# Keeping the second parts of the input projection's weights in DRAM between the two halves of a decoder stack

## The chip, the core and the metric

The kernel runs on one core of one Trainium2 chip. What counts is the device time of one execution in microseconds. Of the kernel before there are three timed runs, 1667.75, 1672.88 and 1679.4 us, with the median 1672.88 us, and one profiled execution of 1675.07 us, whose span in the trace is 1673.3 us.

## What is computed

Two decoder layers run over a prompt of 512 tokens and, beside it, 8 sequences of 4 new tokens each (32 columns more). Per layer the reference does this:

```
h = rms_norm(x, g_mix_pre)
p_rw, p_s5, p_gdn, p_swa = split(h @ w_in)        # the input projection, 1024 -> 2824
o = [rwkv7(p_rw), s5(p_s5), gated_delta(p_gdn), window_attention(p_swa)]
x = x + rms_norm(concat(o) @ w_out, g_mix_post)
h = rms_norm(x, g_mlp_pre)
x = x + rms_norm(square(relu(h @ w_up)) @ w_down, g_mlp_post)
```

All is float32. The four mixers carry state from token to token; the states are outputs too.

## The kernel before, in words

The 544 columns are worked in two halves: half 0 has 256 prompt columns, half 1 the other 256 and the 32 new ones (288 columns). Features lie on the 128 partitions. Half 1 of a layer needs the mixers' states that half 0 left, so the order of the program is: input projection of half 0, mixers of half 0, input projection of half 1, output projection of half 0, mixers of half 1, MLP of half 0, and so on through both layers (`body`, L1787 on). Work of different stages is interleaved.

Every dense product is made exact enough by splitting both operands into a first part `hi` (the value rounded to the type that TensorE takes, float32r) and a second part `lo` (what is left). Three products are summed: hi by hi, hi by lo, lo by hi. For the weights the split is done on the way in, by `load_part` (L1652): a piece of 128 rows by 4 by 128 weights (256 KB) is loaded into a `wraw` buffer by SP's DMA queue (L1658), ScalarE (ACT) casts it into `whi` (through L231), and VectorE (DVE) subtracts `whi` from `wraw` into `wlo` (through L235). There are 5 buffers for `wraw`, and 3 each for `whi` and `wlo`. A unit of 128 output features takes two such pieces and 24 matmuls: for each piece 4 with `whi` by the activations' first part, 4 with `whi` by their second part, and 4 with `wlo` by their first part (`dense`, L1699; matmuls are L219).

The input projection (`project`, L1852) has 22 such units and one narrow one per layer and half, so its 44 pieces are loaded and split four times in the program: layers 0 and 1, halves 0 and 1. Each half loads and splits the same weights anew.

Each unit's result is taken out of PSUM by code of its own mixer. For the first 8 units (`rw_evac`, L367 on) GpSimd (POOL) copies a column into the buffer (L381, L382), ACT copies the result out of PSUM, and POOL keeps the last column in `rwlast` (L398) and another piece in `rwshs` (L386). POOL also adds up squares for the norms (`sums`, L235), and issues some output DMAs from its own queue.

No order is written by hand. The program is recorded in the order of the code, and a scheduler in the build, which times the program by a simulation of its own and takes the priorities in `PRIO` into account, decides in which order the instructions stand on each engine. On the chip each engine, and SP's and POOL's DMA issues among them, goes through its own list in order.

Of the kernel before, what the change touches and what calls it, by code (L numbers as in the profile page):

```python
# [9 lines left out]
F32 = mybir.dt.float32  # L10
F32R = mybir.dt.float32r
# [5 lines left out]
DEPTH, D, SEQ, DB, DS = 2, 1024, 512, 8, 4  # L17
# [121 lines left out]
class K:  # L139
# [1509 lines left out]
        self.nc.sync.dma_start(out=self.x[half], in_=src)  # L1649
        return new  # L1650

    def load_part(self, src):  # L1652

        m = src.shape[-1]
        raw = self.t([128, 4, 128], "wraw", bufs=5)[:, :, :m]
        hi = self.t([128, 4, 128], "whi", bufs=3, dt=F32R)[:, :, :m]
        lo = self.t([128, 4, 128], "wlo", bufs=3, dt=F32R)[:, :, :m]
        d = self.nc.sync.dma_start(out=raw, in_=src)  # L1658
        self.after(d, self.last_load)
        self.last_load = d.ins  # L1660
        self.loads += 1
        if self.loads == FIRST_LOADS:
            for w in self.waiting:
                self.after(w, d.ins)
        self.acopy(hi, raw)
        self.tt(lo, raw, hi.bitcast(F32), ALU.subtract)
        return hi, lo

    def later(self, f):
# [26 lines left out]
        while self.pending:  # L1696
            self.pending.pop(0)()

    def dense(self, units, half, rhs, evac):  # L1699

        n = HALVES[half][1]
        rh, rl = rhs
        for j, (key, src) in enumerate(units):
            if j in (1, 2) and self.pending:
                self.pending.pop(0)()
            ps = self.ps([128, n], "mm")[:src.shape[-1]]
            i = 0
            for k0 in (0, 4):
                with self.ahead("load"):
                    hi, lo = self.load_part(src[:, k0:k0 + 4])  # L1710
                for a, b in ((hi, rh), (hi, rl), (lo, rh)):
                    for k in range(4):
                        self.mm(ps, a[:, k], b[:, k0 + k], i == 0, i == 23)
                        i += 1
            with self.ahead("evac"):
                evac(key, ps)
# [70 lines left out]
    def body(self):  # L1787
        self.pool("sb")
        self.pool("psum", space=PSUM)
        self.pool("dram", space=DRAM)  # L1790
        self.x = [self.i["xT"][:, :, c0:c0 + n] for c0, n in HALVES]
        self.last_layer = False
        self.carry = [{} for _ in range(DEPTH)]
        self.mix = {}
        self.last_gd = None
        self.mean = self.t([128, 1], "mean")
        self.nc.gpsimd.memset(self.mean, 1.0 / D)
        self.eps = self.t([128, 1], "eps")
        self.nc.gpsimd.memset(self.eps, NORM_EPS)
        self.nc.scalar.preload_act_table_set("natural_log_exp_and_others")  # L1800
        h = self.first(0)
        self.tables(0)

        a, b = (self.w([128, 2304], "f9") for _ in range(2))
        xs = self.w([128, 2048], "acc")
        self.alt = dict(xs=xs, cv=a[:, 0:1536], sv=a[:, 1536:1792], gz=b[:, 0:512], us=b[:, 512:1024], sx=b[:, 1024:1792],
                        ba=b[:, 1792:2048])
        r = self.project(0, 0, h)
        zero = self.w([128, 520], "r4")
        self.nc.gpsimd.memset(zero, 0.0)  # L1810
        self.diag = []
        for w in range(2):
            self.diag.append([self.t([64 * 1040], f"diag{w}{x}", pool="dram") for x in range(2)])
            for d in self.diag[w]:
                self.nc.gpsimd.dma_start(out=d.rearrange("(p f) -> p f", p=128), in_=zero)
        self.alt = None
        h = self.first(1)
        self.mixers(r)
        for l in range(DEPTH):
            self.pf = self.pfs[l]  # L1820
            self.last_layer = l == DEPTH - 1
            if not l:
                r = self.project(l, 1, h)
                x = self.out_proj(l, 0)
            else:
                x = self.out_proj(l, 0)
                self.flush()
                r = self.project(l, 1, h["h"])
            self.mixers(r)
            xb = []  # L1830
            other = lambda: xb.append(self.out_proj(l, 1))
            h = self.mlp(l, 0, x, other if l == DEPTH - 1 else None)
            if not xb:
                other()
                self.flush()
            x = xb[0]
            if l + 1 < DEPTH:
                self.tables(l + 1)
                self.pf = self.pfs[l + 1]
                r = self.project(l + 1, 0, h["h"])  # L1840
                self.mixers(r)
                self.pf = self.pfs[l]
            h = self.mlp(l, 1, x)
        self.flush()
# [6 lines left out]

    def project(self, l, half, h):  # L1852
        def proj(us, evac):
            self.dense([(u, self.unit("w_in", l, u)) for u in us], half, h, evac)

        with self.section("rwin"):
            rw = self.rw_begin(l, half)
            proj(range(0, 8), lambda u, ps: self.rw_evac(rw, u, ps))
        with self.section("gdin"):
            gd = self.gd_begin(l, half)  # L1860
            proj((10, 11, 12, 13, 14, 15), lambda u, ps: self.gd_evac(gd, u - 10, ps))
            self.narrow(self.i["w_ba"][l].rearrange("p (k m) -> p k m", k=8), half, h, lambda ps: self.gd_evac_ba(gd, ps))
            proj((16, 17), lambda u, ps: self.gd_evac_z(gd, u - 16, ps))
        with self.section("swin", bank="mm"):
            sw = self.sw_begin(l, half)
            proj((18, 19, 20, 21), lambda u, ps: self.sw_evac(sw, u - 18, ps))
        with self.section("s5in"):
            s5 = self.s5_begin(l, half)
            proj((8, 9), lambda u, ps: self.s5_evac(s5, u - 8, ps))
            us = s5["us"]  # L1870
            s5["sc"] = self.t([256, 4, s5["N"]], f"s5su{half}", pool="dram", bufs=2)
            self.nc.sync.dma_start(out=s5["sc"].rearrange("(u p) j c -> p u (j c)", u=2), in_=us.rearrange("p u j c -> p u (j c)"))
        return dict(l=l, half=half, rw=rw, gd=gd, sw=sw, s5=s5)
# [160 lines left out]
```

## Time and the profile before

| | |
|---|---|
| median of three runs | 1672.88 us |
| profiled execution | 1675.07 us, span 1673.3 us |
| TensorE busy in matmuls (PE) | 1576.6 us, 94% of the span |
| weight loads of TensorE (PEld) | 1472.2 us, 88% |
| VectorE (DVE) | 1245.0 us, 74% |
| ScalarE (ACT) | 952.2 us, 57% |
| GpSimd (POOL) | 373.9 us, 22% |
| DMA | 275.21 MB, 164 GB/s on the mean |

Busy times are those of instructions; a matmul's end is modelled, since matmuls are pipelined. The four input projections lie at about 2 to 112 us (layer 0, half 0), 112 to 250 us (layer 0, half 1), 640 to 725 us (layer 1, half 0) and 1033 to 1119 us (layer 1, half 1), by the starts of the loads `wraw<-in_w_in` in SP's queue.

### The profile page before, as it was taken

What the parts mean: (1) busy time and instruction counts of PE and PEld (TensorE: products, weight loads), DVE (VectorE), ACT (ScalarE), POOL (GpSimd) and SP (SyncE); (2) the same over time, 40 slices, a digit from 0 to 9 for tenths busy, and PEclk for the clock granted to TensorE, in tenths of its full rate; (3) what the DMA queues carried; (4) which work ended last, traced back from release to release, by engine and by line L of the source; (5) the groups of instructions that cost most, each with busy time, mean ns of one, the idle gap of its engine ahead of it and who ended that gap; (6) DMA issues with size and microseconds to landing.
All of it is one profiled execution on the core that took longest, in us unless ns stands there. A gap on an engine that the chain in (4) does not pass through costs nothing. (4 is left out here: it accounts for less than half of the span.)

```text
span 1673.3 us, 38301 instructions
## 1 busy us (share of the span) xinstructions
PE 1576.6 (94%) x14098; PEld 1472.2 (88%) x14098; DVE 1245.0 (74%) x3067; ACT 952.2 (57%) x2096; POOL 373.9 (22%) x689
## 2 busy tenths in 40 slices
PE   6988998789999999989999998999999999899996
PEld 6877987679898999879989998989899899899996
DVE  7888675876696868898576667989778865966665
ACT  5676556744346467765453556886444456655543
POOL 6561142200122614530001004530002101400002
PEclk9998998879999999999999999999999899999998
DMA  6634453343467557736346455535544765555452
GB/s 219 221 120 118 140 165 123 108 119 117 135 189 252 179 170 231 234 105 167 106 152 196 165 179 191 172 126 144 145 140 146 234 209 187 194 189 166 160 169 98
DMA packets 210184, 275.21 MB, mean 164 GB/s; under 512 B 78266, under 2 KB 101116, under 8 KB 209580
## 3 DMA queue, kind: packets, MB, share of 16 engines
q1 hardware_dynamic: 208076, 266.59, 50.8%
q0 software_dynamic: 1920, 6.17, 1.0%
q8 instruction: 110, 1.80, 0.4%
q14 instruction: 78, 0.64, 0.1%
HBM read 243.20 MB, written 31.21 MB: 164 GB/s over the span
## 5 line engine op out<-in xcount | busy, mean ns | idle before, releaser
L231 ACT CAST whi<-wraw 128x512 fp32r<-128x512 f32 x752 | 463.5, 619 | 439.3 <-PE ps L219 268.4
L235 DVE TENSOR_TENSOR wlo<-wraw,whi 128x512 fp32r<-128x512 f32 x752 | 545.7, 730 | 198.5 <-ACT whi L231 171.3
L219 PE MATMUL ps<-h,whi 128*128 128x288 f32 (+1 forms) x3264 | 518.6, 299 | 20.1 <-ACT h L231 17.8
L219 PEld LDWEIGHTS ps<-h,whi 128*128 128x128 f32 x3264 | 455.4, 194 | 35.2 <-ACT h L231 22.1
L219 PE MATMUL ps<-f,whi 128*128 128x288 f32 (+1 forms) x2752 | 425.6, 294 | 9.6 <-ACT whi L231 4.7
L219 PEld LDWEIGHTS ps<-f,whi 128*128 128x128 f32 x2752 | 374.4, 190 | 22.4 <-ACT whi L231 6.8
L219 PE MATMUL ps<-h,wlo 128*128 128x288 f32 (+1 forms) x1632 | 291.0, 298 | 7.4 <-DVE wlo L235 6.8
L219 PEld LDWEIGHTS ps<-h,wlo 128*128 128x128 f32 x1632 | 238.7, 193 | 16.1 <-DVE wlo L235 11.2
L219 PE MATMUL ps<-f,wlo 128*128 128x288 f32 (+1 forms) x1376 | 238.7, 293 | 3.3 <-DVE wlo L235 3.1
L235 POOL TENSOR_TENSOR sums<-sums,d 128x288 f32<-128x288 f32 (+1 forms) x105 | 101.8, 970 | 548.9 <-ACT d L227 541.0
L219 PEld LDWEIGHTS ps<-f,wlo 128*128 128x128 f32 x1376 | 197.4, 190 | 8.5 <-DVE wlo L235 4.6
L219 PE MATMUL ps<-r,r 128*128 128x72 f32 (+7 forms) x800 | 90.0, 281 | 4.5 <-DVE r L235 2.6
L219 PEld LDWEIGHTS ps<-r,r 128*128 128x128 f32 (+4 forms) x800 | 72.3, 175 | 11.0 <-DVE r L235 3.3
L235 DVE TENSOR_TENSOR acc<-acc,ps 128x256 f32<-128x256 f32 (+1 forms) x96 | 41.7, 434 | 49.5 <-PE ps L219 49.1
L231 ACT CAST f<-d 128x256 fp32r<-128x256 f32 (+1 forms) x136 | 56.6, 416 | 29.1 <-DVE d L235 28.5
L227 ACT ACTIVATE d<-acc 128x288 f32<-128x288 f32 (+1 forms) x109 | 46.2, 431 | 34.5 <-DVE acc L235 20.9
L235 DVE TENSOR_TENSOR f<-d,f 128x256 fp32r<-128x256 f32 (+1 forms) x136 | 59.1, 436 | 6.8 <-ACT f L231 6.7
L235 DVE TENSOR_TENSOR d<-d 128x288 f32<-128x288 f32 (+1 forms) x128 | 58.1, 454 | 0.7 <-ACT d L227 0.7
L227 ACT ACT_TABLE_LOAD x43 | 55.2, 1283 | 0.8
L227 ACT ACTIVATE d<-ps 128x288 f32<-128x288 f32 (+1 forms) x128 | 50.4, 394 | 8.8 <-PE ps L219 8.0
L244 DVE SCALAR_TENSOR_TENSOR d<-acc,pf,sums 128x256 f32<-128x256 f32 (+1 forms) x80 | 39.7, 507 | 6.2 <-ACT sums L227 4.9
L231 ACT COPY r<-ps 64x128 f32<-64x128 f32 (+2 forms) x60 | 22.7, 383 | 27.3 <-PE ps L624 11.4
(381 smaller groups left out, 1861.9 us busy)
## 6 DMA issues: line engine op xcount, KB each, us to landing
wraw<-in_w_up SPq DMA_DIRECT2D x256, 256.0 KB, 2.8
wraw<-in_w_down SPq DMA_DIRECT2D x256, 256.0 KB, 2.9
wraw<-in_w_in SPq DMA_DIRECT2D x176, 256.0 KB, 3.0
wraw<-in_w_out SPq DMA_DIRECT2D x64, 256.0 KB, 2.9
r<-s5m SPq DMA_DIRECT2D x12, 512.0 KB, 5.2
t<-diag SPq DMA_DIRECT2D x32, 128.0 KB, 3.2
r<-s5kin SPq DMA_DIRECT2D x8, 512.0 KB, 5.2
x<-acc SPq DMA_DIRECT2D x3, 1152.0 KB, 5.5
```

The source lines that it names most:

```text
L219: return self.nc.tensor.matmul(out=out, lhsT=lhsT, rhs=rhs, start=start, stop=stop)
L227: return self.nc.scalar.activation(out=out, in_=in_, func=func, scale=scale, bias=bias, **kw)
L231: return self.nc.scalar.copy(out, in_)
L235: return (eng or self.nc.vector).tensor_tensor(out=out, in0=a, in1=b, op=op)
L244: return self.nc.vector.scalar_tensor_tensor(out=out, in0=a, scalar=s, in1=b, op0=op0, op1=op1)
```

## The change

In half 0 of each layer, after the subtraction, SP stores each `wlo` piece to a DRAM tensor `kept`, one for each layer. In half 1 no subtraction is done: POOL's DMA queue reads the piece from `kept` into the `wlo` buffer. The load of `wraw` and the cast to `whi` stay in both halves. All other dense products are as they were.

```diff
-    def load_part(self, src):
+    def load_part(self, src, kept=None, first=True):
         ...
         self.acopy(hi, raw)
+        if kept is not None and not first:
+            self.nc.gpsimd.dma_start(out=lo, in_=kept)
+            return hi, lo
         self.tt(lo, raw, hi.bitcast(F32), ALU.subtract)
+        if kept is not None:
+            self.nc.sync.dma_start(out=kept.bitcast(F32), in_=lo.bitcast(F32))
         return hi, lo
 ...
-    def dense(self, units, half, rhs, evac):
+    def dense(self, units, half, rhs, evac, keep=None):
         ...
                 with self.ahead("load"):
-                    hi, lo = self.load_part(src[:, k0:k0 + 4])
+                    kept = None if keep is None else keep[:, key, k0:k0 + 4]
+                    hi, lo = self.load_part(src[:, k0:k0 + 4], kept, not half)
 ...
+        self.kept = [self.t([128, 22, 8, 128], f"kept{l}", dt=F32R, pool="dram") for l in range(DEPTH)]
 ...
         def proj(us, evac):
-            self.dense([(u, self.unit("w_in", l, u)) for u in us], half, h, evac)
+            self.dense([(u, self.unit("w_in", l, u)) for u in us], half, h, evac, self.kept[l])
```

Since the scheduler times the program anew, the order changes on every engine. Three places follow. In the names, the last number is a running number of the tile; `whi` and `wlo` are the pieces of weights, `f` the activations' two parts, `ps` the result in PSUM, `e` the buffer that a unit's result is copied to.

The first place is TensorE in the input projection of layer 1, half 1. Before:

```order
L219 MATMUL ps_14787<-f_2810_14244,wlo_14790 128x288 x4
L219 MATMUL ps_14787<-f_2810_14244,whi_14807 128x288 x4
L219 MATMUL ps_14787<-f_2811_14245,whi_14807 128x288 x4
L219 MATMUL ps_14837<-f_2810_14244,whi_14839 128x288 x4
L219 MATMUL ps_14837<-f_2811_14245,whi_14839 128x288 x4
L219 MATMUL ps_14787<-f_2810_14244,wlo_14808 128x288 x4
L219 MATMUL ps_14837<-f_2810_14244,wlo_14840 128x288 x4
```

Now:

```order
L219 MATMUL ps_14829<-f_2812_14334,wlo_14850 128x288 x4
L219 MATMUL ps_14877<-f_2812_14334,wlo_14880 128x288 x4
L219 MATMUL ps_14877<-f_2812_14334,whi_14897 128x288 x4
L219 MATMUL ps_14877<-f_2813_14335,whi_14897 128x288 x4
L219 MATMUL ps_14977<-f_2812_14334,whi_14979 128x288 x4
L219 MATMUL ps_14977<-f_2813_14335,whi_14979 128x288 x4
L219 MATMUL ps_14877<-f_2812_14334,wlo_14898 128x288 x4
L219 MATMUL ps_14927<-f_2812_14334,wlo_14930 128x288 x4
```

The matmuls with `whi` of the unit after next now stand ahead of those with `wlo`, and the `wlo` groups of two units come as neighbours. The pieces are given to the three `wlo` buffers in turn, in the order 14850, 14880, 14898, 14930: the buffer of 14850 is the one that 14930 is read into, and 24 matmuls stand between the two.

The second place is POOL in the same stretch. Before:

```order
L398 COPY rwlast_9305<-e_2918_14728 128x1
L386 COPY rwshs_9306<-e_2918_14728 128x8
L381 COPY e_2926_14776<-rwlast_9305 128x1
L382 COPY e_2926_14776<-rwshift_9292 128x8
L235 TENSOR_TENSOR sums_14529<-sums_14529,d_2883_14565 128x256
```

Now:

```order
L1667 DMA wlo_14980<-kept_2_64 128x512
L381 COPY e_2944_14964<-rwlast_9351 128x1
L382 COPY e_2944_14964<-rwshift_9338 128x8
L398 COPY rwlast_9351<-e_2936_14914 128x1
L386 COPY rwshs_9352<-e_2936_14914 128x8
L1667 DMA wlo_14998<-kept_2_64 128x512
L1667 DMA wlo_15028<-kept_2_64 128x512
```

The reads of `kept` stand between copies that wait for ACT, and the copies stand behind reads that wait for a free `wlo` buffer.

The third place is SP's queue in the input projection of layer 1, half 0. Before:

```order
L1658 DMA wraw_9663<-in_w_in 128x512
L1658 DMA wraw_9681<-in_w_in 128x512
L1658 DMA wraw_9708<-in_w_in 128x512
L1658 DMA wraw_9726<-in_w_in 128x512
L1658 DMA wraw_9753<-in_w_in 128x512
```

Now:

```order
L1671 DMA kept_2_64<-wlo_9887 128x512
L1658 DMA wraw_10031<-in_w_in 128x512
L1671 DMA kept_2_64<-wlo_9915 128x512
L1658 DMA wraw_10050<-in_w_in 128x512
L1671 DMA kept_2_64<-wlo_9934 128x512
L1658 DMA wraw_10073<-in_w_in 128x512
```

Stores and loads alternate; a load stands behind the store of the piece five before it, whose `wraw` buffer it takes.

## Rows read from the trace of the kernel before

**Rows 1.** The page's first part: busy us (share of the span) xinstructions.
```profile
PE 1576.6 (94%) x14098; PEld 1472.2 (88%) x14098; DVE 1245.0 (74%) x3067; ACT 952.2 (57%) x2096; POOL 373.9 (22%) x689
```

**Rows 2.** The page's chain that ended last, shares by engine.
```profile
PE 41%; DVE 2%; DMA 1%; ACT 1%; POOL 1%; issue 1%; SPq 0%; DVEq 0%; ACTq 0%; POOLq 0%
```

**Rows 3.** Busy time by stretch: the four input projections, a dense stretch, a crowded one.
```profile
core 0: us, PE busy (x) PEld busy (x) DVE busy (x) ACT busy (x) POOL busy (x), PEclk, DMA share, GB/s
20.00:112.00 92.00, 85.62 (x679) 78.31 (x679) 78.56 (x170) 61.43 (x136) 67.76 (x154) 0.96 0.52 176
115.00:250.00 135.00, 127.02 (x1404) 115.09 (x1405) 106.33 (x323) 79.57 (x199) 31.92 (x97) 0.96 0.48 140
640.00:725.00 85.00, 78.62 (x599) 74.09 (x598) 72.41 (x139) 66.69 (x154) 51.52 (x107) 0.98 0.65 211
1045.00:1119.00 74.00, 72.36 (x499) 68.30 (x499) 68.69 (x173) 58.98 (x158) 38.63 (x71) 0.95 0.52 161
1500.00:1600.00 100.00, 100.00 (x755) 100.00 (x755) 59.94 (x108) 49.99 (x97) 0.00 (x0) 1.00 0.51 165
640.00:660.00 20.00, 19.98 (x152) 18.70 (x151) 15.73 (x31) 16.42 (x37) 5.79 (x7) 1.00 0.82 266
```

**Rows 4.** TensorE's waits in 78 to 250 us: us in total, times, longest.
```profile
PE ps L219 <- ACT h L231: 4.8, 3, 2.5
PE ps L219 <- DVE r L235: 2.4, 1, 2.4
PE ps L219 <- ACT e L231: 2.0, 4, 0.7
PE ps L219 <- DVE g L235: 1.0, 1, 1.0
```

**Rows 5.** TensorE's waits in 1030 to 1120 us.
```profile
PE ps L219 <- ACT f L231: 3.8, 2, 3.6
PE ps L219 <- ACT whi L231: 2.1, 3, 1.0
PE ps L219 <- DVE f L235: 0.2, 1, 0.2
```

**Rows 6.** The tile `wlo` in 1045 to 1119 us: ns min/median/max.
```profile
L235 DVE TENSOR_TENSOR wlo<-wraw,whi x38: 672/679/1227, 1046.6 to 1118.9; 128x512 fp32r<-128x512 f32 x38
```

**Rows 7.** DMA issues in 1045 to 1119 us: xcount, KB each, median us from issue to landing.
```profile
wraw<-in_w_in SPq DMA_DIRECT2D x37, 256.0 KB, 2.7
out_conv_s<-gdcs POOLq DMA_DIRECT2D x1, 72.0 KB, 3.0
out_shift_s<-rwshs POOLq DMA_DIRECT2D x1, 32.0 KB, 3.8
out_shift_p<-rwlast POOLq DMA_DIRECT2D x1, 4.0 KB, 4.3
out_conv_p<-gdlast POOLq DMA_DIRECT2D x1, 9.0 KB, 2.6
```

**Rows 8.** DMA issues in 115 to 250 us.
```profile
wraw<-in_w_in SPq DMA_DIRECT2D x41, 256.0 KB, 2.8
out_shift_s<-rwshs POOLq DMA_DIRECT2D x1, 32.0 KB, 3.2
wnar<-in_w_ba SPq DMA_DIRECT2D x1, 32.0 KB, 2.3
out_shift_p<-rwlast POOLq DMA_DIRECT2D x1, 4.0 KB, 2.4
```

**Rows 9.** DMA issues in 640 to 660 us, the crowded stretch.
```profile
wraw<-in_w_in SPq DMA_DIRECT2D x10, 256.0 KB, 3.5
```

**Rows 10.** DMA issues of POOL in 515 to 520 us, five within 4 us.
```profile
out_gd_s<-s POOLq DMA_DIRECT2D x1, 512.0 KB, 7.4
out_swv_s<-c POOLq DMA_DIRECT2D x1, 16.0 KB, 7.2
```

**Rows 11.** Timeline of POOL, layer 1, half 1: start us, us, what.
```profile
1078.69 0.64 POOL L405 DMA_DIRECT2D out_shift_p<-rwlast  x1
```

**Rows 12.** DMA throughput in 640 to 725 us, in 40 slices.
```profile
GB/s 218 212 287 256 384 304 166 280 313 196 139 184 139 312 260 404 314 157 265 265 197 208 177 214 160 156 212 222 163 400 230 362 155 61 90 161 0 0 131 73
DMA packets 11067, 17.91 MB, mean 211 GB/s; under 512 B 2275, under 2 KB 4722, under 8 KB 10928
```

## The prediction

> **What bounds the kernel now.** I read the busy times first. TensorE has matmuls in flight for 94% of the span, DVE is busy for 74%, ACT for 57% [rows 1], and the chain that ended last lies on TensorE far more than on all the others together [rows 2]. The change takes away no matmul, so all that it can win is TensorE's idle time beside the projections of half 1, and the lower clock that goes with it. Next come the stretches [rows 3]. The half-1 projections are the places where DVE loses work: in layer 0 (115 to 250 us) TensorE is idle for 8.0 of 135 us, in layer 1 (1045 to 1119 us) for 1.6 of 74 us, although DVE is busy for 106.3 and 68.7 us there. Then TensorE's waits in slightly wider windows [rows 4, 5]: those on DVE directly are small, 2.4, 1.0 and 0.2 us; those on casts of normed activations (h and f on ACT, which DVE feeds) are 4.8 and 3.8 us; `wlo` is not among the rows. So DVE's subtraction is hidden today. The reader is to see that DVE is loaded, but is not what TensorE waits for.
>
> **What is removed.** 88 subtractions of about 0.68 us [rows 6], 60 us of DVE, 30 in each layer. The waits that DVE has a hand in are 2.4 + 1.0 + 0.2 us directly and 4.8 + 2.0 + 3.8 us through ACT, 14.2 us together [rows 4, 5]. That is the upper end of the direct gain; the lower is nothing, since most of it is a norm's chain at the start of each stage, before many pieces are due. I take 3 us, about a fifth. SP's loads of `wraw` in half 1 no longer wait for DVE, only for ACT's cast; this hides nothing more, since TensorE waits only 2.1 us for `whi` [rows 5].
>
> **What is added in half 1: 88 reads by POOL.** TensorE reads a `wlo` piece last, then POOL sees the free buffer, issues (0.64 us in row [rows 11], which I take to lie inside the time to landing), and the piece lands; only then can the next group with that buffer run. With three buffers the question is how many matmuls stand between the release of a buffer and its next use in the new order. I counted all 44 in layer 1, half 1. Seven have 22 to 28 matmuls (five of them 24 or 25), thirteen have 30 to 33, three 35 to 37, and the other 21 have 40 or more. A dense stretch at full clock runs 755 matmuls in 100 us, 0.132 us each [rows 3]. So the shortest intervals are about 3.2 us, the next 4.2 us, then 5.3 us.
>
> No such read is in the trace, so I bound it. Small transfers of POOL's queue in these very projections land after 2.4 to 4.3 us, and six of them have the mean 3.2 us [rows 7, 8]. On SP's queue 256 KB take 0.5 us more than 32 KB (2.8 against 2.3) [rows 8], and in a crowded stretch (DMA share 0.82 against 0.52) 0.8 us more [rows 3, 7, 9]. This gives 3.2 + 0.5 + 0.8 = 4.5 us, which I take. The low end is 3.2 us; the high end is 7.4 us, when several transfers of POOL follow each other at once [rows 10].
>
> At 4.5 us the seven short intervals lack 1.3 us each and the thirteen 0.3 us, 13 us in all. But a stall also lengthens the intervals of the two other buffers. Going through the 44 uses in order, each stall pushing everything behind it, leaves 2 us at a landing of 3.5, 4 at 4.0, **8 at 4.5**, 13 at 5, 24 at 6 and 38 at 7. In layer 0 the mixers' matmuls stand between the groups: the intervals are 28 to 132 matmuls, 36 of 44 have 38 or more, and the same walk gives 3 us at 4.5, 14 at 6 and 26 at 7. I take 8 + 3 = 11 us.
>
> What is queued behind these reads is on POOL: the copies L381, L382, L398 and L386 and the norm's `sums`. A read behind L398 waits for ACT to empty the PSUM of the unit before, about 1 us. Such a read is the one with the long interval (41 matmuls, 5.4 us, against 4.5 + 1), so I add nothing for it.
>
> **What is added in half 0: 88 stores by SP.** The buffer of `wlo` is now free only when its store has landed, about 3 us after the subtraction by the 256 KB loads. The next subtraction into it is three pieces later: 85 us for 44 pieces give 5.8 us in layer 1, more in layer 0, so this is hidden. SP's order adds no wait, because a load behind the store of piece i already waited for the subtraction of piece i. The bytes count more. In the dense stretch a share of 0.51 moves 165 GB/s [rows 3], so 256 KiB cost 0.81 us of all 16 engines, and 44 stores 36 us. In layer 0, half 0, the share goes from 0.52 to 0.85 or 0.9. In layer 1, half 0, it goes from 0.65 (55 of 85 us) to 91 of 85 us, which would lengthen the stage by 6 us. The slices there reach 400 GB/s [rows 12], while 17.9 + 11.5 MB in 85 us are only 346 GB/s, which would fit. Between 0 and 6 us I take 3. In half 1 of layer 1 the reads add the same 36 us to 38 of 74, which makes exactly 1.0; that is the reason for the 0.8 us above.
>
> **The order.** The scheduler moves work on every engine, in the second layer's mixers and MLP as well. I put it at 0 and at 8 us either way in the range: the idle spots of TensorE in the rest of the program have the same causes, norms and the mixers' chains.
>
> **Sum.** Profiled execution 1675.1 - 3 + 11 + 3 = 1686 us. The median of the runs is 2.2 us below that execution, so the forecast is **1684 us**, 0.7% slower, which counts as no change: differences up to 1% (1656 to 1690 us) are what measurements of this kernel can hardly tell from none.
>
> **A rule that speaks against the change.** POOL's own DMA instruction takes 0.64 us while DVE is busy for 68.7 of 74 us, and POOL's transfers land after 2.6 to 4.3 us there [rows 3, 7, 11], so the trace shows no long hold-up by DVE, and the sum stays 1684 us. The Trainium skill (SBUF — State Buffer, section "SBUF: two separate sides", the warning on DVE blocking DMA) says that GpSimd can't write the descriptors of its DMAs while a VectorE instruction holds both ports of the pair they share, and gives 620 ns alone against 3100 ns beside a copy. An estimate by that page is a landing 2.5 us later, at 7.0 us, and a sum of 1737 us. Its section "Who interferes with whom" exempts instructions with two tensor inputs, which the trace shows to be most of DVE's work here.
>
> **Rivals.**
> *A, the reads land late (chance 0.24).* Place: POOL's queue in half 1. If a landing takes 6 to 7 us, because two reads follow each other in POOL's queue (as 15028 follows 14998), because DMA is full, or because POOL's issue is held up by DVE, the walks give 24 + 14 to 38 + 26 us, so 1711 to 1737 us. It decides from a landing of about 5.2 us (13 + 6 us) on. For it: 7.4 us in [rows 10]. Against it: those five were issued within 4 us, and here at most two are.
> *B, DVE's relief counts (chance 0.18).* The mixers get ahead in half 1, and the waits of 14.2 us go, with some of the lower clock: a mean of 0.96 over 135 us is 8% of the time at the lower level, half of which, 5 us, is lost. With the reads hidden this gives 1672.9 - 14 - 5 = 1654 us at best, and about 1662 with half of it. Against it: TensorE's waits are for norms, not for the mixers' DVE work.
> *C, all is hidden (chance 0.14).* Landing at 3.2 to 3.7 us, DMA not full: 1670 to 1677 us. The change does what it says, so that rival gets nothing.
> *Forecast (chance 0.44):* 1677 to 1695 us.
>
> **Numbers.** Faster by over 1% needs the best of B: 0.07. Slower by over 1% is nearly all of A and a quarter of the forecast's cases (landings near 5 us or an order that costs 5 us more): 0.24 + 0.11 = 0.35. Within 1%: 0.58. The range from 1661 to 1717 us leaves out half of B and the upper part of A, about 0.2.
>
> **What would show it.** Right: DVE has 88 fewer `wlo` instructions; the reads take 4 to 5 us from issue to landing; in the half-1 projection of layer 1 TensorE waits some 8 us for DMAs into `wlo`, in gaps of about 1 us; a stretch near 640 to 725 us whose DMA share is above 0.9 and whose `wraw` lands after 4 us or more. Wrong: landings above 5.5 us with the clock falling below 0.9 in that stretch (A), the waits for h, f and r gone (B), or more than 10 us of change after 1120 us or between 250 and 640 us, where the change itself does nothing (the order).

## The result and the profile after

The changed kernel takes 1728.7 us (median of four runs, 1724.42 to 1733.79) against 1672.1 us for the kernel before in the same comparison: a ratio of 1.0325, interval 1.0292 to 1.0359, some 56 us slower. The forecast was 1684 us and its range ended at 1717 us. Two things make the difference. In one and the same order of instructions the stores and reads, less the subtractions saved, cost 35 us (31 by the ratio), where the prediction's terms came to 11; and the order made for them, which the prediction put at nothing and at most 8 us, costs the change some 20 us more.

From the page of the kernel after, the busy times (as in [rows 1]), the cost group of POOL's issues, and three rows of DMA issues (as in [rows 7], over the whole span):

```profile
PE 1594.6 (93%) x14098; PEld 1479.1 (86%) x14098; DVE 1196.1 (69%) x2979; ACT 958.4 (56%) x2099; POOL 390.4 (23%) x777
...
L1667 POOL DMA_DIRECT2D wlo<-kept x88 | 49.1, 558 | 133.6 <-PE ps L219 112.3
...
wraw<-in_w_in SPq DMA_DIRECT2D x176, 256.0 KB, 4.3
kept<-wlo SPq DMA_DIRECT2D x88, 256.0 KB, 3.7
wlo<-kept POOLq DMA_DIRECT2D x88, 256.0 KB, 4.3
```

The 88 subtractions are gone (2979 DVE instructions against 3067) and DVE is busy for 48.9 us less. TensorE does the same 14098 matmuls in 18.0 us more of busy time, and its idle time rose from 96.7 to 128.1 us; these two make the 49.4 us by which the spans differ (1722.7 against 1673.3 us). A read of `kept` lands 4.3 us after its issue. What TensorE waits for, over the whole span, after (us in total, times, longest):

```profile
PE ps L219 <- DVE wlo L235: 34.2, 26, 7.7
PE ps L219 <- DMA wlo<-kept: 10.5, 8, 2.6
PE ps L219 <- ACT h L231: 10.4, 8, 3.6
PE ps L219 <- ACT whi L231: 9.4, 11, 2.9
```

and the same rows of the kernel before:

```profile
PE ps L219 <- ACT h L231: 17.8, 10, 3.6
PE ps L219 <- DVE wlo L235: 9.8, 12, 1.5
...
PE ps L219 <- ACT whi L231: 6.5, 9, 1.2
```

The reads cost TensorE 10.5 us in 8 waits, which is what the prediction had worked out (11 us). What grew most is another row: the waits for DVE's own `wlo` subtractions, 34.2 us against 9.8, although DVE has less to do. The stretches of the kernel after, columns as in [rows 3] (the start, layer 1 half 0, layer 1 half 1, a dense one):

```profile
0.00:60.00 60.00, 44.04 (x301) 37.79 (x302) 43.22 (x107) 32.23 (x70) 33.40 (x90) 1.00 0.84 285
660.00:762.00 102.00, 86.21 (x608) 79.03 (x607) 77.47 (x155) 74.30 (x166) 48.11 (x109) 0.95 0.83 282
1067.00:1170.00 103.00, 86.64 (x571) 78.47 (x571) 55.30 (x149) 75.28 (x187) 53.74 (x119) 0.97 0.80 245
1549.00:1649.00 100.00, 100.00 (x755) 100.00 (x754) 59.80 (x108) 50.32 (x98) 0.00 (x0) 1.00 0.50 166
```

The first three of the kernel before, the projections cut at the same points of the program:

```profile
0.00:60.00 60.00, 46.38 (x328) 41.52 (x329) 48.38 (x118) 35.40 (x77) 37.89 (x93) 1.00 0.67 218
640.00:727.00 87.00, 80.19 (x608) 75.39 (x606) 74.41 (x144) 68.67 (x156) 52.31 (x109) 0.98 0.65 213
1033.00:1120.00 87.00, 80.78 (x559) 75.48 (x558) 76.72 (x184) 68.86 (x182) 47.70 (x79) 0.96 0.55 172
```

The two projections of layer 1 now take 102 and 103 us instead of 87 each, with nearly the same matmuls, and TensorE is idle for about 16 us in each instead of 6 to 7. The dense stretch is untouched. Both stages also carry more DMA, so from this profile alone late buffers, full DMA or the order could each be the cause.

To see where time is lost or won back, I read in SP's queue when the first load of each weight tensor's next phase is issued. The table gives, for the profiled executions, how many us later than before that is.

| first load of | before, at us | after | stores only | reads only | before in new order | change in old order | the same, 4 buffers |
|---|---|---|---|---|---|---|---|
| layer 0, MLP of half 0 | 301 | 18 | 10 | 13 | 15 | 19 | 12 |
| layer 1, half 0 `w_in` | 641 | 20 | 10 | 18 | 15 | 22 | 11 |
| layer 0, MLP of half 1 | 727 | 35 | 28 | 18 | 28 | 31 | 17 |
| layer 1, half 1 `w_in` | 1033 | 34 | 27 | 16 | 26 | 30 | 15 |
| layer 1, MLP of half 0 | 1120 | 50 | 27 | 34 | 48 | 39 | 16 |
| its second `w_up` | 1200 | 65 | 27 | 51 | 67 | 40 | 16 |
| last `w_down` | 1622 | 50 | 25 | 39 | 52 | 39 | 17 |

The last five columns are experiments told below. These are single executions: "before in new order" ends 52 us late here, and its median is 60 us above. It does the work of the kernel before and follows the column "after" roughly, with 22 us lost in layer 1's half-1 projection (26 to 48) against 16 (34 to 50).

### The profile page after: what moved, and what is told of

Its sections match the earlier page's. It is cut to its first block, busy times and chain, and to the rows that moved or that the text cites. A ratio compares the mean times of both kernels' runs of the same rounds, so it can differ in the third digit from the quotient of the medians.

```text
span 1722.7 us, 38565 instructions
## 1 busy us (share of the span) xinstructions
PE 1594.6 (93%) x14098; PEld 1479.1 (86%) x14098; DVE 1196.1 (69%) x2979; ACT 958.4 (56%) x2099; POOL 390.4 (23%) x777
## 5 line engine op out<-in xcount | busy, mean ns | idle before, releaser
L235 DVE TENSOR_TENSOR wlo<-wraw,whi 128x512 fp32r<-128x512 f32 x664 | 479.4, 725 | 208.2 <-ACT whi L231 171.5
L235 POOL TENSOR_TENSOR sums<-sums,d 128x288 f32<-128x288 f32 (+1 forms) x105 | 98.4, 938 | 568.3 <-ACT d L227 566.3
L1667 POOL DMA_DIRECT2D wlo<-kept x88 | 49.1, 558 | 133.6 <-PE ps L219 112.3
L235 DVE TENSOR_TENSOR acc<-acc,ps 128x256 f32<-128x256 f32 (+1 forms) x96 | 41.8, 435 | 44.4 <-PE ps L219 44.3
L235 DVE TENSOR_TENSOR f<-d,f 128x256 fp32r<-128x256 f32 (+1 forms) x136 | 61.7, 455 | 9.8 <-ACT f L231 9.6
L235 DVE TENSOR_TENSOR d<-d 128x288 f32<-128x288 f32 (+1 forms) x128 | 60.4, 472 | 0.0
```

The lines of the kernel that those rows point to most:

```text
L235: return (eng or self.nc.vector).tensor_tensor(out=out, in0=a, in1=b, op=op)
L1667: self.nc.gpsimd.dma_start(out=lo, in_=kept)
```

## The experiments

Theories at the start: *late reads* (three buffers, the read occupies one for its landing), *bytes* (DMA full), *queue and buffer* (a store holds SP's queue and its buffer), and *order*. Differences in us are of medians, against the kernel before in the same comparison (its medians were 1672.1 to 1675.4 us). From e9 to e16 the line numbers are shifted by four: L223 is the matmul, L239 the subtraction, L235 a cast or copy by ACT.

**One part alone.** The stores without the reads, and the reads without the stores.

```diff
 e1_stores_only
-        if kept is not None and not first:
-            self.nc.gpsimd.dma_start(out=lo, in_=kept)
-            return hi, lo
...
-        if kept is not None:
+        if kept is not None and first:
 e2_reads_only (the weights themselves are read into lo: same bytes, no second part)
-            self.nc.gpsimd.dma_start(out=lo, in_=kept)
+            self.nc.gpsimd.dma_start(out=lo, in_=src)
-        if kept is not None:
-            self.nc.sync.dma_start(out=kept.bitcast(F32), in_=lo.bitcast(F32))
```

> Half 0 stores its second parts as in the change, half 1 subtracts as before and reads nothing back (the stored pieces are not used). Theory L (late reads: the 44 reads of each layer through three buffers are the cost): the stores alone cost under 10 us, 1673 to 1682 us. Theory B (bytes: 44 stores of 256 KB in an 85 us stage fill the DMA engines): 20 to 35 us, near 1700 us, with wraw landing after 4.3 us or more in half 0. Theory Q (each store holds a second-part buffer and stands in SP's one queue ahead of the next load): also 20 to 35 us; it differs from B in the next run but one.

> No stores. In half 1 POOL's queue fills each second-part buffer with 256 KB straight from the weights in DRAM, so the second parts of half 1 are the weights themselves. Theory L: 40 to 56 us slower, near 1720 us. Theories B and Q: the reads cost 15 to 25 us, since 56 us less the stores is what is left; 1688 to 1700 us. If the parts add up to far less than 56 us (both within 10 us of before), neither is the cause, and the order that the scheduler made of the whole is.

Measured: stores 1701.9 us, ratio 1.0153 (1.0119 to 1.0188), +27; reads 1708.6 us, 1.0193 (1.0156 to 1.0230), +34. Together 61, the change 56: the two parts seem to add up, each for the most part in its own stages (table). Stores that were to cost 3 us cost 27, reads that were to cost 11 cost 34.

**Fewer bytes.** A quarter of each piece is stored, then 16 bytes a partition.

```diff
 e3_stores_quarter (otherwise as e1)
-            self.nc.sync.dma_start(out=kept.bitcast(F32), in_=lo.bitcast(F32))
+            self.nc.sync.dma_start(out=kept.bitcast(F32)[:, 0:1], in_=lo.bitcast(F32)[:, 0:1])
 e5_stores_tiny (otherwise as e1)
-            self.nc.sync.dma_start(out=kept.bitcast(F32), in_=lo.bitcast(F32))
+            self.nc.sync.dma_start(out=kept[:, 0, :4].bitcast(F32), in_=lo[:, 0, :4].bitcast(F32))
```

> As the run with stores alone, but each store moves only the first of the piece's four 128-column blocks, 64 KB in place of 256 KB; the number of stores, their place in SP's queue and the buffers they hold are the same. Theory B: the cost falls to a quarter, 1675 to 1682 us. Theory Q: most of the cost stays (the landing of a small store is still 2 us or more), within 8 us of the run with whole stores.

> Before with the 88 stores of half 0 alone, each of 2 KB (16 bytes a partition) instead of 256 KB; nothing reads them. The stores of 256 KB gave 1702 us, those of 64 KB 1691, before 1675. Theory bytes (the stores' traffic delays the loads): 1672 to 1680, since 0.2 MB are nothing. Theory queue and buffer (the store waits on SP's queue for the subtraction and holds the second part until it has landed, whatever its size; a 64 KB store still took 2.6 us to land): 1683 to 1692. Theory order (the program of the engines is re-sorted by the scheduler whenever a step is added): anything from 1665 to 1695, with the change of time not in the stages where the stores are.

Measured: 1691.4 us, 1.0088 (1.0052 to 1.0125), +17, and 1698.5 us, 1.0150 (1.0106 to 1.0194), +24. 88 stores of 2 KB, 0.2 MB, cost nearly as much as 23 MB, and 1698.5 us lies outside what each theory had wanted. But the equal totals are not the same loss. By the starts of the loads in SP's queue, e5 is level with before at 245 us and 21 us late at 301 us, a stretch in which nothing is stored; e1 is 10 us late at 301 us and loses 18 us in layer 1, half 0. The scheduler had drawn a new order for each. So these two runs don't price the traffic. A 2 KB store still takes 2.5 us to land (256 KB: 3.5 us in e1), so queue and buffer were not excluded either.

**Another queue.** The whole change, read back by SP instead of POOL.

```diff
-            self.nc.gpsimd.dma_start(out=lo, in_=kept)
+            self.nc.sync.dma_start(out=lo.bitcast(F32), in_=kept.bitcast(F32))
```

> The whole change, but SP's queue in place of POOL's reads the pieces back. Theory L with POOL's queue as its cause (slow landing, copies ahead of it): 20 to 35 us faster than the change, about 1695 to 1710 us. If the three buffers and the bytes are the cause and not the queue: within 8 us of the change, 1720 to 1737 us; slower than the change if SP's single queue, now with two DMAs for each piece, holds the loads up.

Measured: 1728.5 us, 1.0302 (1.0265 to 1.0340), the time of the change, with a landing of 3.7 instead of 4.3 us. Reading by SP wins nothing back in all. That POOL's queue costs nothing does not follow, since this order is a new one too and loses at other places: by SP's queue, layer 1's half-1 projection loses 7 us here and 16 in the change, its half-0 projection 22 and 15.

**Another order of the same work.** Nothing but the rank of the load steps changes.

```diff
-PRIO = {... 'load': 294, ...}
+PRIO = {... 'load': 304, ...}
```

> Before with one number of the scheduler's table changed, the rank of the load steps 294 to 304, so that a part of TensorE's order in layer 0 and a little in layer 1 is sorted anew and nothing is added or removed. Theory order (a new order of the same work costs tens of us): at least 8 us away from 1673. Theories queue, buffer and bytes: within 8 us of 1673 (1665 to 1681).

Measured: 1683.9 us, 1.0061 (1.0032 to 1.0090), +10. An order alone can cost what I had allowed for it at most.

**A fourth buffer**, first in the scheduler's own orders: a control with the work of before, and the change.

```diff
-        lo = self.t([128, 4, 128], "wlo", bufs=3, dt=F32R)[:, :, :m]
+        lo = self.t([128, 4, 128], "wlo", bufs=4, dt=F32R)[:, :, :m]
-            Sn = self.t([128, 2, 64], "rwS", bufs=5)
+            Sn = self.t([128, 2, 64], "rwS", bufs=4)
```

> Before with a fourth buffer for the second parts; the space comes from the recurrence's state buffers, five to four. It is the control of the next run. All theories: 1660 to 1685; TensorE's waits for the subtractions (16 us in the two half-1 stages of before) fall to under 10 us if the three buffers were what spaced them.

> The whole change with a fourth buffer for the second parts (and four state buffers, as in the control). Theory buffer (a second part occupies its buffer for the landing of 4.3 us instead of a subtraction of 0.7, and in half 0 until the store has landed): the distance to the control falls from 56 us to 10 to 30. Theory bytes: the distance stays 45 to 60. Theory queue (the store's wait on SP holds back the loads behind it): the half-0 part of the distance, about 27, stays, the half-1 part falls, together 30 to 40.

Measured: control 1691.4 us, 1.0095 (1.0063 to 1.0127), +17; change 1703.0 us, 1.0185 (1.0129 to 1.0241), +29. The distance to the control is 12 us, as the buffer theory has it, but the control itself lost 17 us. With the order drawn anew in each kernel neither number could be trusted. (The 16 us of waits that the first expectation names have no row behind them: over the whole span before, TensorE waits 9.8 us for `wlo`.)

**Order and content taken apart.** So I held the order. The kernel's own instructions of all engines are listed as they were recorded, and each is made to follow its neighbour in a given order, by a dependency that sets the order and no wait. Free are only the stores, the reads, and the 88 subtractions of half 1 where they exist; the scheduler places these.

```diff
+    def fix_order(self):
...
+        for ins in self.nc.cur_bb.bb.instructions:
+            if ins.name not in self.free:
+                mine.setdefault(str(ins.engine).split(".")[-1], []).append(ins)
...
+            for a, b in zip(o, o[1:]):
+                self.tc.add_manual_dep(mine[e][b], mine[e][a].name, self.NOSYNC, reason="order")
```

> The whole change, but every other instruction of TensorE, VectorE, ScalarE, GpSimd and SP is held in the order of before by order-only dependencies between neighbours; the scheduler places only the 88 stores and 88 reads. Theory order (what costs is the new order): 1672 to 1685. Theory buffers (stores and reads occupy the three buffers for 3.5 to 4.3 us a piece, in any order): 1715 to 1740. Both in part: about 1700.

> Nothing is stored or read back: the work of before, with its subtractions, held in the order that the scheduler made for the change. Theory order: 1710 to 1730, the time of the change. Theory buffers: 1668 to 1685. Both in part: about 1700. It tells also whether the two causes add up with the run before.

> The stores alone (256 KB each, as in the change), everything else in the order of before. With the scheduler's own order they gave 1702, and stores of 2 KB 1699. Theory order: 1670 to 1682. Theory queue and buffer: 1690 to 1705, the loss in the half-0 projections.

> The reads alone (256 KB of the weights themselves read into the second part's buffer in place of each subtraction of half 1, so its output isn't the reference's), everything else in the order of before. With the scheduler's own order they gave 1709. Theory order: 1670 to 1682. Theory buffers: 1700 to 1715, the loss in the half-1 projections, most of it in layer 1.

| | work of before | stores | reads | stores and reads |
|---|---|---|---|---|
| in the order of before | 0 | +13 | +27 | +35 |
| in the scheduler's own order for that work | 0 | +27 | +34 | +56 |

Measured: e9 1709.0 us, 1.0188 (1.0148 to 1.0228); **e10 1734.0 us, 1.0333 (1.0289 to 1.0376), +60**; e11 1687.7 us, 1.0082 (1.0054 to 1.0109); e12 1701.7 us, 1.0123 (1.0065 to 1.0181; 21 us by the ratio, 27 by the medians).

Two pairs are clean, since they hold the order or the instructions fixed. The change in the order of before takes 35 us more than before. The same change in its own order takes 20 us more than that (1728.7 against 1709.0 us, intervals of the ratios apart). Together they make up the 56.

The other way round, the work of before is as slow as the change once it is put in the order made for it, and stores and reads, which cost 35 us in the old order, cost nothing that can be measured in the new one. That fits an order which makes room for slow pieces at a price of its own: in the change DVE waits 2.8 us for stores and TensorE 10.5 us for reads, in e9 11.3 and 15.5 us. But e10 is not the order alone. In half 1 its DVE does 88 subtractions that the change does not have, in an order made without them. So its 60 us may be more than the order's price, and which of the two prices is the larger is not settled.

How an order loses time is seen in e10. TensorE's waits over its whole span:

```profile
PE ps L223 <- DVE wlo L239: 27.0, 22, 3.0
PE ps L223 <- ACT h L235: 10.3, 8, 3.6
PE ps L223 <- ACT whi L235: 10.2, 10, 3.5
...
PE ps L223 <- ACT xs L231: 6.6, 4, 2.5
```

The waits for `wlo` are there (27.0 us) with no store in the program: in this order the subtractions come later than TensorE wants them. None of the 27.0 us lies in the half-1 projections, so the subtractions put back are not their cause. In the half-0 projection of layer 1 and the mixers behind it, in the change, in e10 and before:

```profile
PE ps L219 <- DVE wlo L235: 10.0, 7, 2.8
PE ps L223 <- DVE wlo L239: 9.0, 6, 2.8
PE ps L219 <- DVE wlo L235: 0.7, 1, 0.7
```

There e10 loses 13 us (15 to 28) and the change 15 (20 to 35), with the same lists on every engine but for the stores: this loss is the order's. The two layer-1 projections of e10, as above:

```profile
655.00:758.00 103.00, 89.72 (x614) 82.24 (x614) 80.78 (x159) 75.32 (x168) 49.30 (x111) 0.92 0.58 182
1059.00:1168.00 109.00, 89.81 (x575) 81.43 (x574) 81.30 (x191) 75.75 (x190) 37.84 (x80) 0.94 0.45 137
```

In the second TensorE is idle for 19 of 109 us, with DVE and ACT idle for 28 and 33, a DMA share of 0.45, and a granted clock of 0.94: no engine is full, they wait for each other. One such place, ACT's timeline and then TensorE's (start us, us, what, idle time before it):

```profile
1109.73 0.40 ACT L235 CAST h<-d 128x256 fp32r<-128x256 f32 x1 [1.09 <-DVE d L248]
1110.04 0.61 ACT L235 CAST whi<-wraw 128x512 fp32r<-128x512 f32 x1
1110.59 0.40 ACT L235 CAST h<-d 128x256 fp32r<-128x256 f32 x1
1110.90 0.46 ACT L235 COPY e<-ps 128x256 f32<-128x256 f32 x2
1111.24 0.67 ACT L231 ACTIVATE xs<-ps,rwd 128x32 f32<-128x32 f32 x2
```

```profile
1108.76 0.69 PE L223 MATMUL ps<-f,wlo 128*128 128x288 f32 x4
1111.96 1.33 PE L223 MATMUL ps<-f,whi 128*128 128x288 f32 x4 [2.51 <-ACT xs L231]
```

The next unit's matmuls need a PSUM result that ACT has yet to copy out (`e`, `xs`). ACT's list has two casts of the norm of half 0 (`h`, 256 columns) ahead of the copies, and one of them waits for DVE. So TensorE stands still for 2.51 us for copies of about 1 us. In the kernel before, the timeline at a like place has the copies ahead of `whi` and `h`, and TensorE did not wait for them:

```profile
1077.75 0.48 ACT L231 COPY e<-ps 128x256 f32<-128x256 f32 x2
...
1078.08 0.71 ACT L227 ACTIVATE xs<-ps,rwd 128x32 f32<-128x32 f32 x2
...
1078.62 0.68 ACT L231 CAST whi<-wraw 128x512 fp32r<-128x512 f32 x1
...
1079.13 0.78 ACT L231 CAST h<-d 128x256 fp32r<-128x256 f32 x2
```

In e10 ACT in turn waits for TensorE to leave a `whi` buffer (its row in that stage, 7.3 us in 5 waits, against 2.0 us before):

```profile
ACT whi L235 <- PE ps L223: 7.3, 5, 4.5
```

This second place is e10's own. The change has the same list on ACT, but waits for other things in that projection. The change, then e10:

```profile
PE ps L219 <- DMA wlo<-kept: 8.1, 6, 2.6
PE ps L219 <- ACT whi L231: 4.4, 3, 2.9
```

```profile
PE ps L223 <- ACT xs L231: 6.6, 4, 2.5
PE ps L223 <- ACT whi L235: 6.3, 4, 3.5
```

DVE is busy there for 81.30 us in e10 and 55.30 in the change, and one of the subtractions put back stands just before the `d` that the late cast waits for:

```profile
1108.62 0.68 DVE L239 TENSOR_TENSOR wlo<-wraw,whi 128x512 fp32r<-128x512 f32 x1
...
1109.22 0.47 DVE L248 SCALAR_TENSOR_TENSOR d<-acc,pf,sums 128x256 f32<-128x256 f32 x1
```

So e10's 22 us in this projection may in part be these subtractions. Of the change's 16 us there, 8.1 are TensorE's waits for reads.

**Buffers, with the order held.** The four buffers of e8 once more, now in the order of before.

> The whole change in the order of before, with a fourth buffer for the second parts (state buffers of the recurrence five to four). With three buffers it was 1709, 35 over before. Theory buffers (a piece keeps its buffer from the issue of the read to the last matmul, and the store keeps it in half 0): 1675 to 1690, since every read may start one piece earlier. Theory bytes or queues (DMA full, or SP's and POOL's queues late, whatever the buffers): 1700 to 1715.

> Control of the run before: the work of before in the order of before, with four buffers for the second parts and four state buffers. All theories: 1668 to 1678, as before; the four-buffer control in the scheduler's own order was 1691, so if this is 1674, those 17 were order and not the state buffers.

Measured: control 1673.8 us, 1.0007 (0.9979 to 1.0034); change 1688.9 us, 1.0091 (1.0060 to 1.0123), +16. The control shows that holding the order costs nothing, that the fourth buffer and the lost state buffer matter little, and that the 17 us of e7 were order. Of the change's 35 us in the old order 19 go with one more buffer. The half-1 projection of layer 1 in the old order, with three buffers (9 us longer than before):

```profile
1063.00:1159.00 96.00, 82.18 (x556) 75.83 (x555) 53.62 (x144) 69.82 (x181) 54.43 (x119) 0.96 0.87 262
```

and its wait for the reads in that stretch:

```profile
PE ps L223 <- DMA wlo<-kept: 8.9, 6, 3.2
```

With four buffers it takes 88 us, 1 more than before:

```profile
1048.00:1136.00 88.00, 79.75 (x554) 73.89 (x552) 52.81 (x144) 68.93 (x179) 53.72 (x120) 0.98 0.94 289
```

```profile
PE ps L223 <- DMA wlo<-kept: 2.6, 4, 0.9
```

```profile
wlo<-kept POOLq DMA_DIRECT2D x41, 256.0 KB, 5.1
```

DMA is busier there (0.94), the reads land later (5.1 us in this stretch), and yet the loss is gone. In this order late reads and three buffers were that stage's mechanism; bytes were not. What remains with four buffers is lost before 301 us (12 us) and in layer 1, half 0 (6 us). In e11, the stores in the old order, the first 60 us have a DMA share of 0.89 against 0.67:

```profile
0.00:60.00 60.00, 43.88 (x298) 38.94 (x299) 45.43 (x112) 33.70 (x73) 32.78 (x92) 1.00 0.89 296
```

and DVE waits for stores to leave the three buffers, 12.0 us over the span:

```profile
DVE wlo L239 <- DMA kept<-wlo: 12.0, 10, 3.6
```

With four buffers that wait of DVE is down to 2.4 us, so the hold on the buffer is not what remains. In its first 108 us e13 falls 6 us behind, with loads landing after 4.9 us (3.4 before). The other 6 us come in layer 0, half 1, where TensorE waits 4.0 us for `t<-diag` and 2.6 us for `r<-s5sz`, DMAs of the mixers (0.6 us together before, no such row in e14). Both point to the fuller DMA or to SP's longer list; no run with small stores in the old order tells these apart.

**Which part makes the order that costs?** The work of before in the order of e1 and of e2.

> The work of before, nothing stored, in the order that the scheduler made for the stores alone. Stores in their own order 1702 (27 over before), in the old order 1688 (13 over). Theory order first (an order made for slower buffers costs by itself, and the stores then cost nothing more in it): 1695 to 1705. Theory sum (own order = order + mechanism): 27 - 13 = 14 over, 1685 to 1692.

> The work of before, with its subtractions, in the order that the scheduler made for the reads alone. Reads in their own order 1709 (34 over), in the old order 1702 (27 over). Theory order first: 1700 to 1712, lost in layer 1, half 1, where only the order differs. Theory sum: 34 - 27 = 7 over, 1676 to 1686.

Measured: 1698.8 us, 1.0151 (1.0096 to 1.0206), +26, and 1716.8 us, 1.0263 (1.0203 to 1.0323), +44. Each part's order, without the part, costs as much as the part did with it (27 and 34). The theory that own order is order plus mechanism falls: it wanted +14 and +7. For the stores this is clean, since e15 has the same instructions as before. e16, like e10, has 88 subtractions more than its order was made for; it lies 8 us above the reads' own time and above what either theory allowed.

**A bad draw?** The change with the loads ranked at 304 and 340 instead of 294.

> The whole change with the rank of the load steps 304 instead of 294, so that the scheduler sorts anew. If the bad order is chance (a draw that another rank would change, as the same step moved before by 10): over 12 us away from 1729, 1690 to 1716 or above 1742. If the reads and stores make every order of this scheduler bad alike: 1717 to 1741.

> The same with the rank 340, which lets loads stand further ahead. Chance: over 12 us away from 1729 or from the run at 304. Bad alike: 1717 to 1741. If loads further ahead give the reads the time they lack: below 1710.

Measured: 1733.3 us, 1.0341 (1.0318 to 1.0364), and 1725.9 us, 1.0299 (1.0252 to 1.0345). Three orders for the change lie within 8 us of each other and 50 to 58 us above before. So it does not look like a bad draw: given these stores and reads, this scheduler made such an order three times. Why it does is open. The argument would be that its own timing sees the pieces late and therefore puts work of other stages ahead of them; no run here looks into that timing.

No version beat the kernel before.

## Why the prediction was wrong, step by step

- **What bounds the kernel** held in the main: 31 of the 49 us are TensorE's idle time, and the dense stretches are unchanged. The other 18 us are longer busy time for the same matmuls, which the prediction had no term for (last section).
- **The removal, 3 us of gain**, shows nowhere. DVE lost 48.9 us of work, but even with the reads nearly hidden (e13) the half-1 projection of layer 1 took 88 us against 87. The 14.2 us of waits that I took a fifth of [rows 4, 5] belong to norms, as rival B's counter-argument said: TensorE's wait for `f` is 3.8 us in e13's stretch, too.
- **The reads' landing, 4.5 us**: right, 4.3 us. **The walk, 8 + 3 us**: right for what it described, 8.1 us of waits for `kept` in layer 1, half 1, and 10.5 in all. But it is a wait counted in the new order, without that order's price. In the order of before the reads cost 21 to 27 us (e12), and TensorE waits 17.2 us for them.
- **POOL's copies behind reads, 0**: not settled. Moving the reads to SP leaves the total as it is, but in another order (e4).
- **The stores, 3 us** was mis-sized: 13 us in the old order (e11). The hold on the buffer, which I called hidden because a stage's mean interval is 5.8 us, shows as 12.0 us of DVE's waits; and I priced the bytes in layer 1 alone. For layer 0, half 0, I foresaw the higher share (in the first 60 us it rose from 0.67 to 0.89) and priced nothing.
- **The order, 0 and 8 us either way**: this is the step that failed. It was argued from where TensorE idles before, "the same causes, norms and the mixers' chains". For the change itself the order costs 20 us (e9 against the change, same instructions), for the stores' order without the stores 26 us (e15), and in e10, with the reservation above, 60. With the stores and reads at 35 us in place of 11, the 20 us make up the whole miss. I had read in the new order that `whi` matmuls moved ahead and `wlo` groups became neighbours, used it for the reads alone, and did not ask whether the subtractions of half 0 and of the other products still come in time for TensorE: its waits for them grew from 9.8 to 34.2 us.
- **Rival A** (1711 to 1737 us) holds the measured time by another mechanism: the reads land at 4.3 us, not 6 to 7. **The rule weighed** goes the same way: 558 ns for an issue by POOL and 4.3 us to landing, with DVE busy for 55.3 of 103 us. The Trainium skill (SBUF — State Buffer, section "SBUF: two separate sides") would have had descriptors held up by DVE and, as an estimate, landings of 7.0 us; no row here shows that. SP's queue, which that page recommends instead, landed the reads at 3.7 us and gave the same time of the kernel, in another order.
- My sign for the order, "more than 10 us of change where the change itself does nothing", was met: between 1120 and 1200 us the loss grows from 50 to 65 us, in e10 from 48 to 67, and about 15 of it are won back later.
- My signs for being right were met too: 88 subtractions fewer, reads at 4.3 us, 8.1 us of waits for them in layer 1, half 1, and a DMA share of 0.92 at 700 to 720 us in a stage whose loads land after 4.3 us. They tested the reads and the bytes in the new order. None of them tested what that order costs, so they came true beside a time 45 us above the forecast.

## What to carry to other kernels

Where a scheduler sorts the program anew, an edit has two prices: what the new instructions cost, and what the order made for them costs. The second can be as large as the first or larger; test it by running the old work in the new order and the new work in the old one. Best compare runs with the same instructions, since an order can also suffer from instructions that it was not made for (e10, e16). A comparison of sizes, queues or buffer counts in which each kernel gets its own order says little below about 20 us here (e4 to e7), and equal totals can hide losses at different places. With the order held it is sharp (e14 at 1.0007).

## What the runs showed of the hardware

A store of 2 KB on SP's queue took 2.5 us to land and one of 256 KB 3.5 us, so a small transfer still holds its buffer for over two thirds of the time of a large one. The Trainium skill (DMA: Bandwidth & Descriptors, section "Anatomy of one DMA — SWDGE (gpsimd) path") has a fixed part of 2.0 us for POOL's transfers, which makes 2.6 us for 256 KB as an estimate; POOL's reads here took 4.3 us, among loads that themselves went from 3.0 to 4.3 us. A stretch of 88 us ran at a DMA share of 0.94 and 289 GB/s and lost 1 us, once there was a buffer more. The granted clock over the span hardly moved in the profiled executions, 0.966 before, 0.965 after and 0.963 in e10. Over all timed runs it did: the medians are 0.970 before (in e10's comparison), 0.9625 after and 0.956 in e10. With the lower level at half the clock, an estimate from these means and times is 100, 130 and 153 us at the lower level, so at most 15 us of the change's 56 and 26 of e10's 60 are the clock's, less where TensorE was idle at that level. In e10's two projections it fell together with the pauses (0.92 and 0.94 against 0.98 and 0.96 before); in the change it was 0.95 and 0.97. Whether the pauses bring it down was not tested. In the profiled executions the same estimate gives 114 us at the lower level before and 121 after, which makes only 3 or 4 of the 18 us of longer busy time; the rest of these 18 us is not explained.
